# A mixture-of-experts stage whose experts branch at the fifth weight tile, with split weight tiles that come free one at a time

## The chip, the cores and the metric

The kernel runs on one core of one Trainium2 chip and computes one whole layer of a diffusion backbone in one launch. The metric is the device time of that launch in microseconds (us). Three runs of the kernel before gave 2664.49, 2667.15 and 2668.33 us; the median, 2667.15, is the time before. The trace comes from one more execution.

PE is the matrix engine, DVE the vector engine, ACT the scalar engine, POOL the GpSimd engine, and SP the engine that issues most DMAs.

## What the kernel computes

A layer has a mixing part (neighbourhood attention and a convolution), which the change does not touch, and a mixture of experts on 2048 tokens of 1024 numbers, all in float32:

```python
g_idx = argmax(h @ w_rg + b_rg)                     # one of 4 groups
top_v, top_i = top_k(e_logits in that group, 2)     # 2 of its 8 experts
gate = p_group * softmax(top_v)
for e in range(32):                                 # rows sorted by expert
    xb = h[rows of e]                               # rows x 1024
    y = (silu(xb @ w_g[e]) * (xb @ w_u[e])) @ w_d[e]  # 1024 x 512, 512 x 1024
    out[rows of e] += y * gate
x = x_mid + g2 * out
return rmsnorm(x, final_norm)
```

How many rows an expert gets is known only at run time.

## The kernel before

`stage_moe` takes the 32 experts in order. An expert has 12 weight tiles of 128 x 1024 float32, 512 KB each: tiles 0 to 7 are the gate and up weights (`w_gu`), tiles 8 to 11 the down weights (`w_d`). SP issues the DMA of each (`fetch`, L1207) into a ring of 9 raw buffers `ws`. A raw tile is then split in two by `load` (L1212): ACT copies it to a rounded high part `wh` (L1222), and DVE subtracts that from the raw tile for the low part `wl` (L1224); POOL does the subtraction for 2 of the 12 tiles, gate/up tile 1 and down tile 2 (`POOL_LO`). The split tiles have three sets of buffers, by the letter in their names: five pairs `wha/wla` for gate/up tiles 0 to 2, five `whb/wlb` for tiles 3 to 7, and four `whd/wld` for the down tiles.

A float32 product is three matmuls: high by high, high by low, low by high. `block` (L1316) computes an expert's first 128 rows: 24 matmuls of 512 columns for tiles 0 to 3 into one PSUM tile `g`, 24 for tiles 4 to 7 into another, each closed by a SiLU on ACT (L1342) and a gated product on DVE (L1343), then 24 for the down tiles into `y`. `turn` transposes the 512 intermediate numbers per row, half at a time, and splits them into `pah` and `pal`; `rows_t` does the same for the next expert's rows, between the gate/up and the down matmuls. `split` (L52, L53) is the helper: the high part on ACT, the low part on DVE, out of PSUM. Which load stands behind which matmul is written out by hand in the dictionary `mid`, and the order in the program is the order on each engine, since the stage runs under `manual_schedule`. An engine works its list in order: an instruction that waits holds up all that stands behind it.

An expert can have more than 128 rows. `nblk[e]` counts blocks of 64. After `block`, PE, ACT, DVE and POOL branch (`more{e}`, L1499): for at most two blocks they only run `results` (the PSUM tiles `y` times a gain, added to DRAM rows by POOL's indirect DMA); for three, `block64` computes the further 64 rows against the same 12 tiles; for four, `second` runs `block` again; beyond that there is a loop. In this input, among experts 0 to 30, 19 have at most two blocks ("usual" below), 9 have three (experts 2, 4, 10, 14, 15, 16, 19, 26, 29) and 3 have four (12, 13, 27). Expert 31 is written apart, with the final norm behind it. The further rows `yo` are gathered for each expert that has some, and transposed in every expert at L1375 (`rows_t64`), by the hook `mid[10]`.

Of the kernel before, what the change touches and what calls it, by code (L numbers as in the profile page):

```python
# [21 lines left out]
GB, DB, WS = 5, 4, 9  # L22
# [4 lines left out]
POOL_LO = (("g", 1), ("d", 2))  # L27
# [14 lines left out]
class Net:  # L42
# [827 lines left out]
    def stage_out(self, merging):  # L870
# [9 lines left out]
        with ExitStack() as st:  # L880
# [228 lines left out]
            def first_rows(m, pb):  # L1109
# [15 lines left out]
                self.x0 = _f(self.wr_pool.tile([128, D], F32R, name="wha", bufs=GB))  # L1125
# [81 lines left out]
    def fetch(self, d, e, n):  # L1207
        f = self.wr_pool.tile([128, D], F32, name="ws", bufs=WS)
        self.SY.dma_start(out=f, in_=self.I["w_gu" if d is self.WG else "w_d"][e, n])
        self.raw[d is self.WG, e, n] = f  # L1210

    def load(self, d, e, n):  # L1212

        A, V, P = self.A, self.V, self.P
        gu = d is self.WG
        if (gu, e, n) not in self.raw:
            self.fetch(d, e, n)
        f = self.raw.pop((gu, e, n))
        pool, tag, bufs = (self.wr_pool, "a", GB) if gu and n < 3 else (self.wl_pool, "b", GB) if gu else (self.wl_pool, "d", DB)
        h = pool.tile([128, D], F32R, name="wh" + tag, bufs=bufs)  # L1220
        l = pool.tile([128, D], F32R, name="wl" + tag, bufs=bufs)
        A.activation(out=h, in_=f, func=AF.Copy)  # L1222
        eng = P if ("g" if gu else "d", n) in POOL_LO else V
        eng.tensor_tensor(out=l, in0=f, in1=_f(h), op=OP.subtract)  # L1224
        d.setdefault(e, {})[n] = h, l

    def first_weights(self):

        self.wr_pool = self.ctx.enter_context(self.tc.tile_pool(name="mr", bufs=1, side="right"))
        self.WG, self.WD, self.raw = {}, {}, {}  # L1230
        for n in range(3):
            self.load(self.WG, 0, n)
        for n in range(3, 8):
            self.fetch(self.WG, 0, n)
        for n in range(4):
            self.fetch(self.WD, 0, n)

    def stage_moe(self):
# [4 lines left out]
        with ExitStack() as st:  # L1243
            cp = st.enter_context(tc.tile_pool(name="mc", bufs=1))
            wp = self.wl_pool = st.enter_context(tc.tile_pool(name="mw", bufs=1))
            sp = self.wr_pool
            p = st.enter_context(tc.tile_pool(name="mt", bufs=2))
            tp = st.enter_context(tc.tile_pool(name="mtp", bufs=4, space=PSUM))
            gp = st.enter_context(tc.tile_pool(name="mgp", bufs=2, space=PSUM))
# [26 lines left out]
            yo = cp.tile([128, D], F32, name="yo")  # L1276
            P.memset(yo, 0.0)
            yt = cp.tile([128, D], F32, name="yt")
            yq = [yp.tile([128, CW], F32, name=f"y{half}") for half in range(2)]
            yw = cp.tile([64, D], F32, name="yw")  # L1280
            WG, WD, load = self.WG, self.WD, self.load
# [5 lines left out]
            def rows_t(x, to=None):  # L1287

                xh, xl = to or [p.tile([128, 8, 128], F32R, name=n, bufs=1) for n in ("xh", "xl")]

                def step(b):
                    t = tp.tile([128, 4, 128], F32, name="t")
# [23 lines left out]
            def block(e, x, idx, w, mid={}, between=(), z=None):  # L1316


                xh, xl = x
                at = lambda n: [f() for f in mid.get(n, ())]  # L1320

                def turn(half):
                    t = tp.tile([128, 4, 128], F32, name="t")
                    for k in range(2):
                        T.transpose(t[:, k, :], ps[:, half * 256 + k * 128:half * 256 + (k + 1) * 128], ident)
                    ks = slice(2 * half, 2 * half + 2)
                    self.split(pah[:, ks, :], pal[:, ks, :], t[:, 0:2, :])

                for half in range(2):
                    q = gp.tile([128, 2, 256], F32, name="g")  # L1330
                    for n in range(4):
                        h, l = WG[e][4 * half + n]
                        for j in range(2):
                            k, c = 2 * n + j, slice(j * CW, (j + 1) * CW)
                            T.matmul(q, xh[:, k, :], h[:, c], start=(k == 0), stop=False)  # L1335
                            T.matmul(q, xh[:, k, :], l[:, c], start=False, stop=False)  # L1336
                            T.matmul(q, xl[:, k, :], h[:, c], start=False, stop=(k == 7))  # L1337
                        at(4 * half + n)
                        if half and n == 2:
                            turn(0)  # L1340
                    a = ps[:, half * 256:half * 256 + 256]
                    A.activation(out=a, in_=q[:, 0, :], func=AF.Silu)  # L1342
                    V.scalar_tensor_tensor(out=a, in0=a, scalar=w, in1=q[:, 1, :], op0=OP.mult, op1=OP.mult)  # L1343
                for f in between:
                    f()
                y, qs = yt, yq
                for k in range(4):
                    h, l = WD[e][k]
                    for half, q in enumerate(qs):
                        c = slice(half * CW, (half + 1) * CW)  # L1350
                        T.matmul(q, pah[:, k, :], h[:, c], start=(k == 0), stop=False)
                        T.matmul(q, pah[:, k, :], l[:, c], start=False, stop=False)
                        T.matmul(q, pal[:, k, :], h[:, c], start=False, stop=(k == 3))
                    if k == 0:
                        turn(1)
                    at(8 + k)

                def results():
                    V.tensor_tensor(out=y[:, 0:CW], in0=qs[0], in1=g2r[:, 0:CW], op=OP.mult)
                    A.activation(out=y[:, CW:D], in_=qs[1], func=AF.Copy)  # L1360
                    P.tensor_tensor(out=y[:, CW:D], in0=y[:, CW:D], in1=g2r[:, CW:D], op=OP.mult)
                    if z is None:
                        add_rows(y, 128, idx)
                    else:
                        V.tensor_tensor(out=y, in0=y, in1=z, op=OP.add)

                return results

            def rows_t64(x):

                for b in range(2):
                    t = tp.tile([128, 4, 128], F32, name="t")
                    ks = slice(4 * b, 4 * b + 4)
                    for k in range(4):
                        T.transpose(t[:, k, :], x[:, (b * 4 + k) * 128:(b * 4 + k + 1) * 128], ident)  # L1375
                    self.split(xo[:, ks, 0:64], xo[:, ks, 64:128], t[:, :, 0:64])

            def block64(e, idx, w, z=None, y=None, aside=()):


                def pair(q, s, h, l, first, last):

# [319 lines left out]
```

## Time and profile before

| | us |
|---|---|
| median of three runs | 2667.15 |
| the profiled execution | 2663.24 |
| its span, first to last instruction | 2661.2 |
| experts 0 to 30, first gate matmul 1731.64 to that of expert 31 | 848.1 |
| from expert 31 to the end of the span | 81.4 |
| PE busy in the span | 2421.3 (91%) |
| DVE busy | 1702.9 (64%) |
| ACT busy | 1217.4 (46%) |
| POOL busy | 956.1 (36%) |

The shares are means over stages that differ. The change touches the stretch from 1731.64 on, and so the rows below are of that stretch. In a row of a timeline the first number is the start and the second the duration; consecutive instructions of one form are put together with their count (x2). Matmuls overlap their neighbours by part of their duration, so steps are read from start to start. The bracket at the end is the time that the engine idled before the row, and what ended the idling. [...]

### The profile page before, as it was taken

The numbers are of one execution on the slowest core, as the hardware profiler recorded it, in microseconds if no ns is written. First come the engines' busy times: TensorE is split into PE (matmuls) and PEld (weight loads), VectorE is DVE, ScalarE is ACT, GpSimd is POOL, SyncE is SP. The second block draws the span as 40 slices with busy tenths as digits, with TensorE's granted clock in tenths as the row PEclk, the third lists the DMA queues.
The fourth block names the chain that finished last, engine by engine and source line by source line (L and its number), as shares of the span: only waits on it lengthen the run. The fifth ranks groups of instructions, "written<-read, shape, count | busy, mean of one in ns | idle before, by whom it ended". The sixth has DMA issues, their size and how long they took to land. (4 is left out here: it accounts for less than half of the span.)

```text
span 2661.2 us, 36529 instructions
## 1 busy us (share of the span) xinstructions
PE 2421.3 (91%) x12776; PEld 2005.7 (75%) x12776; DVE 1702.9 (64%) x2687; ACT 1217.4 (46%) x2089; POOL 956.1 (36%) x691
## 2 busy tenths in 40 slices
PE   7997999999999999999889999789999998988992
PEld 3786877788878898888877888677777777777772
DVE  7652079999303033887676666676876667777676
ACT  6511111111125211888763333365765556666564
POOL 2300022332110213667533333344454444444442
PEclk9998999999999999999999999899999999999996
DMA  6488534222434357786736343588897678898786
GB/s 247 148 286 189 151 115 138 66 81 98 153 121 152 102 175 229 166 180 146 161 106 210 127 141 113 186 269 294 301 358 258 208 228 279 264 337 304 242 280 240
DMA packets 239637, 522.16 MB, mean 196 GB/s; under 512 B 31383, under 2 KB 122663, under 8 KB 235751
## 3 DMA queue, kind: packets, MB, share of 16 engines
q1 hardware_dynamic: 177431, 403.50, 43.2%
q0 software_dynamic: 24992, 92.06, 15.3%
q10 hardware_dynamic: 36912, 22.92, 3.3%
q8 instruction: 148, 2.42, 0.4%
q14 instruction: 154, 1.26, 0.2%
HBM read 409.76 MB, written 131.43 MB: 203 GB/s over the span
## 5 line engine op out<-in xcount | busy, mean ns | idle before, releaser
L242 PE MATMUL pj<-hTh,wl 128*128 128x512 f32 x1216 | 475.0, 391 | 9.3 <-POOL wl L173 9.3
L240 PE MATMUL pj<-hTh,wh 128*128 128x512 f32 x1216 | 476.1, 392 | 3.2 <-ACT wh L172 3.2
L241 PE MATMUL pj<-hTl,wh 128*128 128x512 f32 x1216 | 475.9, 391 | 0.0
L300 DVE SCALAR_TENSOR_TENSOR cacc<-u,conv_w,cacc 128x2048 f32<-128x2048 f32 x120 | 311.3, 2618 | 1.9
L173 POOL TENSOR_TENSOR wl<-wf,wh 128x1024 fp32r<-128x1024 f32 x32 | 103.5, 3235 | 559.9 <-ACT wh L172 559.9
L242 PEld LDWEIGHTS pj<-hTh,wl 128*128 128x128 f32 x1216 | 232.6, 191 | 55.8 <-POOL wl L173 11.0
L240 PEld LDWEIGHTS pj<-hTh,wh 128*128 128x128 f32 x1216 | 232.6, 191 | 48.4 <-ACT wh L172 3.6
L241 PEld LDWEIGHTS pj<-hTl,wh 128*128 128x128 f32 x1216 | 232.3, 191 | 44.3 <-DVE hTl L232 0.4
L1224 DVE TENSOR_TENSOR wlb<-ws,whb 128x1024 fp32r<-128x1024 f32 x160 | 184.2, 1214 | 0.0
L1224 DVE TENSOR_TENSOR wld<-ws,whd 128x1024 fp32r<-128x1024 f32 x96 | 151.5, 1605 | 20.9 <-ACT whd L1222 20.4
L1222 ACT ACTIVATE whb<-ws 128x1024 fp32r<-128x1024 f32 x160 | 154.8, 1046 | 0.0
L1224 POOL TENSOR_TENSOR wla<-ws,wha 128x1024 fp32r<-128x1024 f32 x32 | 85.2, 2661 | 187.6 <-ACT wha L1222 180.5
L53 DVE TENSOR_TENSOR PTl<-t,PTh 128x384 fp32r<-128x384 f32 (+2 forms) x256 | 122.4, 519 | 31.0 <-ACT PTh L52 28.4
L1335 PE MATMUL g<-wha,xh 128*128 128x512 f32 x192 | 87.8, 457 | 59.1 <-ACT whb L1222 24.1
L700 DVE CUSTOM_DVE_ANT_0 sb<-s,W 128x640 f32<-128x640 f32 (+1 forms) x128 | 113.8, 890 | 37.0 <-PE s L696 14.1
L1224 DVE TENSOR_TENSOR wla<-ws,wha 128x1024 fp32r<-128x1024 f32 x64 | 104.4, 1631 | 43.5 <-ACT wha L1222 39.1
L318 ACT ACTIVATE sg<-pj 128x512 f32<-128x512 f32 x64 | 37.9, 595 | 204.5 <-PE pj L242 103.0
L1224 POOL TENSOR_TENSOR wld<-ws,whd 128x1024 fp32r<-128x1024 f32 x32 | 92.9, 2903 | 98.7 <-ACT whd L1222 98.7
L1222 ACT ACTIVATE whd<-ws 128x1024 fp32r<-128x1024 f32 x128 | 128.0, 1051 | 0.0
L1335 PE MATMUL g<-whb,xh 128*128 128x512 f32 x320 | 127.7, 399 | 0.0
L1337 PE MATMUL g<-whb,xl 128*128 128x512 f32 x320 | 125.3, 392 | 0.0
L1336 PE MATMUL g<-wlb,xh 128*128 128x512 f32 x320 | 124.8, 390 | 0.0
(417 smaller groups left out, 6304.6 us busy)
## 6 DMA issues: line engine op xcount, KB each, us to landing
ws<-in_w_gu_dram SPq DMA_DIRECT2D x256, 512.0 KB
ws<-in_w_d_dram SPq DMA_DIRECT2D x128, 512.0 KB
wf<-in_w_in_dram SPq DMA_DIRECT2D x32, 512.0 KB
wmod<-in_w_mod_t_dram SPq DMA_DIRECT2D x32, 512.0 KB
vw_s<-v_s ACTq DMA_DIRECT2D x128, 128.0 KB
v<-vw_s POOLq DMA_DIRECT2D x32, 512.0 KB, 3.9
kk<-k_s POOLq DMA_DIRECT2D x16, 576.0 KB, 9.2
h_s<-xn SPq DMA_DIRECT2D x17, 512.0 KB
```

The lines of the kernel that those rows point to most:

```text
L53: self.V.tensor_tensor(out=lo, in0=src, in1=_f(hi), op=OP.subtract)
L173: P.tensor_tensor(out=l, in0=f, in1=_f(h), op=OP.subtract)
L240: T.matmul(p[:, :n], w[0][:, k, :], hTh[c][:, k, :], start=(k == 0), stop=False)
L241: T.matmul(p[:, :n], w[0][:, k, :], hTl[c][:, k, :], start=False, stop=False)
L242: T.matmul(p[:, :n], w[1][:, k, :], hTh[c][:, k, :], start=False, stop=(k == 7))
L300: V.scalar_tensor_tensor(out=acc, in0=u[:, t:t + S], scalar=cw[:, i, t:t + 1], in1=acc, op0=OP.mult, op1=OP.add)
L700: V.tensor_tensor_reduce(out=sb[:, 0:w], in0=s.rearrange("p a b -> p (a b)")[:, 256:256 + w], in1=t.rearrange("p a b -> p (a b)"), scale=1 ...
L1222: A.activation(out=h, in_=f, func=AF.Copy)
L1224: eng.tensor_tensor(out=l, in0=f, in1=_f(h), op=OP.subtract)
L1335: T.matmul(q, xh[:, k, :], h[:, c], start=(k == 0), stop=False)
L1336: T.matmul(q, xh[:, k, :], l[:, c], start=False, stop=False)
L1337: T.matmul(q, xl[:, k, :], h[:, c], start=False, stop=(k == 7))
```

## The change

An expert becomes two pieces of program. The head computes gate/up tiles 0 to 3 and, behind their first tile, writes the results of the expert before. Then comes a branch: an expert of at most two blocks runs `arm` without an argument, one of three `arm(..., Few)`, one of four or more `arm(..., Many)`. An arm does the rest of the expert. In `Few` and `Many` the further rows meet each weight tile soon after the first 128 rows did, in PSUM tiles of their own. The weights 12e + n of all experts now form one sequence; tile t is split into pair t mod 8, so a pair is written again as soon as the tile 8 before it has been used for the last time. There are 20 raw buffers (9 until the stage starts). Five tiles of the next expert are split ahead (`AHEAD`) where two were. `yo` has two buffers, and its transposes are in `Few` and `Many` alone. The same two of an expert's 12 tiles go to POOL (1 and 10). More than four blocks run the slow loop, which this input does not reach. Expert 31 keeps its form, with its loads listed anew.

```diff
-GB, DB, WS = 5, 4, 9
+NP, NP0, WS, WS0 = 8, 4, 20, 9
+AHEAD = 5
-POOL_LO = (("g", 1), ("d", 2))
+POOL_LO = (1, 10)
...
+    def load(self, hl=None):
+        f = self.raw.pop(self.loaded)
+        h, l = hl or self.pairs[self.loaded % NP]
+        self.A.activation(out=h, in_=f, func=AF.Copy)
+        eng = self.P if self.loaded % 12 in POOL_LO else self.V
+        eng.tensor_tensor(out=l, in0=f, in1=_f(h), op=OP.subtract)
+        self.idle.append(f)
+        self.W[self.loaded] = h, l
+        self.loaded += 1
...
+            def arm(e, x, steps, other=None):
+                o, w = other, slot[:, e, 1:2]
+                turns[0] = 0
+                if o:
+                    o.start(e)
+                for n in range(4, 8):
+                    gate_up(gb, x, e, n)
+                    if n == 6:
+                        turn(ps, pah, pal, 0)
+                    if n == 7:
+                        act(gb, ps, 1, w)
+                    if o:
+                        o.gate_up(gc, e, n - 4)
+                    self.load()
+                if o:
+                    o.act(e, gc, 0)
+                for f in steps:
+                    f()
+                if o:
+                    for n in range(4, 8):
+                        o.gate_up(ga, e, n)
+                        self.load()
+                        if n == 5:
+                            turn(ps, pah, pal, 1)
+                        if n == 6:
+                            o.turn(0)
+                    o.act(e, ga, 1)
+                for k in range(4):
+                    down(yq, pah, pal, e, k)
+                    if not o and k == 0:
+                        turn(ps, pah, pal, 1)
+                    if o and k == 1:
+                        o.turn(1)
+                    if not o:
+                        self.load()
+                        if k == 2:
+                            self.load()
+                if o:
+                    for k in range(4):
+                        o.down(qo, e, k)
+                        if k == 1:
+                            self.load()
...
+            def results_of(e):
+                results(yt, yq, ids[:, e:e + 1])
+                n = beyond(e, (mybir.EngineType.Pool, mybir.EngineType.Activation, mybir.EngineType.DVE))
+                with tc.If(n > 2):
+                    with tc.If(n <= 3) as few:
+                        results64(yw, qo, ido[0:64, e:e + 1])
+                    with few.Else():
+                        results(yw, qo, ido[:, e:e + 1])
...
+            for e in range(NE - 1):
+                while self.idle and self.fetched < 12 * NE:
+                    self.fetch()
+                hint(f"usual{e}", nblk[e] <= 2)
+                for n in range(4):
+                    gate_up(ga, x, e, n)
+                    if n < 3:
+                        self.load()
+                    if n == 0:
+                        rest(e + 1)
+                        if e + 2 < NE:
+                            xg[e + 2] = new(e + 2)
+                        if e:
+                            results_of(e - 1)
+                act(ga, ps, 0, slot[:, e, 1:2])
+                nx, steps = rows_t(xg.pop(e + 1))
...
+                with tc.If(nblk[e] <= 2, label=f"usual{e}", preferred_fallthrough_block=True):
+                    hint(f"further{e}", nblk[e] > 2)
+                    arm(e, x, steps)
+                with tc.If(nblk[e] > 2, label=f"further{e}", preferred_fallthrough_block=True):
+                    with tc.If(nblk[e] <= 3):
...
+                        arm(e, x, steps, Few)
+                    with tc.If(nblk[e] > 3, label=f"many{e}", preferred_fallthrough_block=True):
...
+                        arm(e, x, steps, Many)
```

Of the changed code, `gate_up`, `down` and `turn` are the matmuls and transposes of `block` as functions of a tile (L1347 to L1349 and L1355), `act` its SiLU and product (L1371, L1372), `Few` the products of `block64` on the further 64 rows, `Many` those of `block` on the further 128.

On DVE, before, a usual expert ends like this, from the transposed rows of the next expert (`xl`) to its results (`yt`); `wld` is its last down tile, `wla` tile 0 of the next expert:

```order
L53 TENSOR_TENSOR xl<-t,xh 128x512 [waits Activation_49] x2
L53 TENSOR_TENSOR pal<-t,pah 128x256 [waits Activation_49]
L1224 TENSOR_TENSOR wld<-ws,whd 128x1024 [waits DMAHW1_49,Activation_49]
L1224 TENSOR_TENSOR wla<-ws,wha 128x1024 [waits DMAHW2_49,Activation_49]
L53 TENSOR_TENSOR xo<-t,xo 128x4x64 [waits Activation_49] x2
L1499 COMPARE_AND_BRANCH
L1359 TENSOR_TENSOR yt<-y_15941,g2r 128x512 [waits DMASW1_49,DVE_49,DMASW6_49,PE_49,DMASW7_49,Pool_49]
```

After the change the same stretch of a usual expert's arm on DVE reads as follows; `wl_15372`, `wl_15376`, `wl_15378` and `wl_15972` are tiles 0, 2, 3 and 4 of the next expert (tile 1 is POOL's), and the last rows are the end of the arm:

```order
L54 TENSOR_TENSOR xl<-t_15951,xh 128x512 [waits Activation_49]
L54 TENSOR_TENSOR xl<-t_15949,xh 128x512 [waits Activation_49]
L54 TENSOR_TENSOR pal<-t_15950,pah 128x256 [waits Activation_49]
L1222 TENSOR_TENSOR wl_15372<-ws_4_15366,wh_15371 128x1024 [waits DMAHW1_49,Activation_49]
L1222 TENSOR_TENSOR wl_15376<-ws_6_15368,wh_15375 128x1024 [waits DMAHW3_49,DVE_49,Activation_49]
L1222 TENSOR_TENSOR wl_15378<-ws_7_15369,wh_15377 128x1024 [waits DMAHW4_49,DVE_49,Activation_49]
L1222 TENSOR_TENSOR wl_15972<-ws_8_15370,wh_15971 128x1024 [waits DMAHW5_49,DVE_49,Activation_49]
L1637 UNCONDITIONAL_BRANCH
L1637 UNCONDITIONAL_BRANCH [waits DVE_49]
L1640 COMPARE_AND_BRANCH
```

Two splits of weights stood behind `pal`, then those of the further rows and `yt`; now four splits of weights stand there, and `yt` has moved into the next head.

On PE, before, the rows from the last down matmul of an expert past its branch (the code for more rows is left out) to the first gate matmul of the next:

```order
L1352 MATMUL y_15942<-wld,pah 128x512
L1353 MATMUL y_15942<-whd,pal 128x512
L1499 COMPARE_AND_BRANCH
...
L1499 UNCONDITIONAL_BRANCH [waits PE_49]
L1494 REGISTER_ALU
L1698 BRANCH_PREFETCH_HINT
L1454 UNCONDITIONAL_BRANCH
L1335 MATMUL g<-wha,xh 128x512 [waits DVE_49,PE_49,Activation_49]
```

After the change the same place, from the end of the usual arm past the arms for further rows:

```order
L1348 MATMUL y_15947<-wl_15989,pah 128x512
L1349 MATMUL y_15947<-wh_15988,pal 128x512
L1637 UNCONDITIONAL_BRANCH
L1637 UNCONDITIONAL_BRANCH [waits PE_49]
L1640 COMPARE_AND_BRANCH
...
L1640 UNCONDITIONAL_BRANCH [waits PE_49]
L1589 UNCONDITIONAL_BRANCH
L1606 REGISTER_ALU
L1849 BRANCH_PREFETCH_HINT
L1347 MATMUL g_15952<-wh_15371,xh 128x512 [waits DVE_49,Activation_49]
```

PE passes two conditional branches per expert where it passed one, and the first gate matmul behind the join still stands behind waits on DVE and ACT.

In the middle of an expert with three blocks PE now runs from the last matmul of the head past the usual arm to the transposes of the further rows:

```order
L1349 MATMUL g_15952<-wh_15988,xl 128x512
L1637 COMPARE_AND_BRANCH
...
L1637 UNCONDITIONAL_BRANCH
L1637 UNCONDITIONAL_BRANCH [waits PE_49]
L1640 COMPARE_AND_BRANCH
L1641 COMPARE_AND_BRANCH
L1606 REGISTER_ALU
L1849 BRANCH_PREFETCH_HINT
L1407 MATMUL t_15950<-ident,yo_15938 128x128 [waits DMASW5_49,DVE_49]
```

Those transposes stood in `mid[10]`, behind the third down tile; they now stand directly behind the branch, with a wait on DVE, and the gate matmuls of tiles 4 to 7 behind them.

## Rows read from the trace of the kernel before

**Rows 1.** What PE waited for in the stretch 1731.6 to 2579.76
```profile
PE g L1335 <- ACT whb L1222: 24.1, 8, 3.2
PE g L1335 <- PEq L1499: 15.9, 5, 4.3
PE y L1353 <- DVE pal L53: 10.8, 17, 1.1
PE g L1335 <- ACT yt L1360: 10.6, 13, 0.8
```

**Rows 2.** Timeline of PE: start, duration, instruction, idle before and releaser
```profile
1902.06 1.04 PE L1294 MATMUL t<-ident,xg 128*128 128x128 f32 x8
...
1904.32 0.38 PE L1325 MATMUL t<-ident,ps 128*128 128x128 f32 x2
...
1907.29 1.03 PE L1375 MATMUL t<-ident,yo 128*128 128x128 f32 x8
...
1910.54 0.50 PE L1335 MATMUL g<-wha,xh 128*128 128x512 f32 x1 [0.81 <-ACT yt L1360]
...
1974.42 0.75 PE L1335 MATMUL g<-wha,xh 128*128 128x512 f32 x1 [4.26 <-PEq L1499]
```

**Rows 3.** Timeline of ACT in the same expert
```profile
1902.26 0.38 ACT L1342 ACTIVATE ps<-g 128x256 f32<-128x256 f32 x1 [0.96 <-PE g L1337]
...
1902.70 1.09 ACT L52 ACTIVATE xh<-t 128x512 fp32r<-128x512 f32 x2
...
1904.78 0.38 ACT L52 ACTIVATE pah<-t 128x256 fp32r<-128x256 f32 x1 [1.00 <-ACT xh L52]
...
1906.01 2.00 ACT L1222 ACTIVATE wha<-ws 128x1024 fp32r<-128x1024 f32 x2
...
1909.89 0.60 ACT L1360 ACTIVATE yt<-y 128x512 f32<-128x512 f32 x1 [1.14 <-PEq L1499]
```

**Rows 4.** Windows, the 19 usual experts: length, busy times, clock, DMA share, GB/s; one, and sum
```profile
1910.54:1930.38 19.84, 19.03 (x92) 15.44 (x92) 16.25 (x19) 15.28 (x22) 11.54 (x6) 1.00 1.03 377
...
sum 413.22, PE 377.12 PEld 302.19 DVE 331.84 ACT 278.42 POOL 198.77; mean PE 19.85 PEld 15.90 DVE 17.47 ACT 14.65 POOL 10.46
```

**Rows 5.** Windows, the 9 experts with three blocks: third of them, and sum
```profile
1974.42:2009.85 35.43, 32.45 (x161) 25.78 (x161) 21.87 (x31) 21.53 (x35) 11.95 (x7) 0.95 0.78 249
...
sum 315.97, PE 285.56 PEld 225.85 DVE 208.68 ACT 190.35 POOL 142.74; mean PE 31.73 PEld 25.09 DVE 23.19 ACT 21.15 POOL 15.86
```

**Rows 6.** Windows, the 3 experts with four blocks
```profile
2030.11:2068.71 38.60, 37.52 (x176) 30.22 (x177) 21.81 (x26) 17.77 (x27) 15.42 (x9) 1.00 0.74 248
...
sum 118.93, PE 115.16 PEld 92.26 DVE 64.34 ACT 52.01 POOL 46.16; mean PE 38.39 PEld 30.75 DVE 21.45 ACT 17.34 POOL 15.39
```

**Rows 7.** Windows, the gate and up products of two experts, 43 matmuls each
```profile
1890.69:1900.45 9.76, 9.76 (x43) 7.95 (x43) 8.83 (x9) 8.86 (x10) 5.69 (x5) 1.00 0.95 246
1974.42:1985.72 11.30, 11.30 (x43) 9.10 (x44) 9.74 (x9) 8.66 (x10) 2.92 (x3) 0.85 1.04 332
```

**Rows 8.** Timeline of DVE in two usual experts
```profile
1878.50 4.54 DVE L1224 TENSOR_TENSOR wld<-ws,whd 128x1024 fp32r<-128x1024 f32 x2
...
1899.24 2.35 DVE L1224 TENSOR_TENSOR wld<-ws,whd 128x1024 fp32r<-128x1024 f32 x2
...
1903.33 1.29 DVE L53 TENSOR_TENSOR xl<-t,xh 128x512 fp32r<-128x512 f32 x2 [0.17 <-ACT xh L52]
...
1905.20 0.42 DVE L53 TENSOR_TENSOR pal<-t,pah 128x256 fp32r<-128x256 f32 x1 [0.58 <-ACT pah L52]
...
1908.43 0.78 DVE L53 TENSOR_TENSOR xo<-t,xo 128x256 fp32r<-128x256 f32 x2
```

**Rows 9.** Timeline of POOL beside them
```profile
1879.44 2.52 POOL L1224 TENSOR_TENSOR wld<-ws,whd 128x1024 fp32r<-128x1024 f32 x1 [3.79 <-ACT whd L1222]
...
1899.87 3.99 POOL L1224 TENSOR_TENSOR wld<-ws,whd 128x1024 fp32r<-128x1024 f32 x1 [3.48 <-ACT whd L1222]
...
1908.08 2.67 POOL L1224 TENSOR_TENSOR wla<-ws,wha 128x1024 fp32r<-128x1024 f32 x1 [4.23 <-ACT wha L1222]
```

More of the change, by code (lines that the diff above doesn't have):

```diff
@@ L1238, in stage_moe @@
+        self.room(self.wr_pool, WS0, NP0)
+        for _ in range(3):
+            self.fetch()
+        for _ in range(3):
+            self.load()
+        while self.idle:
+            self.fetch()
     def stage_moe(self):
@@ L1314, in put_rows @@
                 return P.indirect_dma_start(out=self.out[:, :], out_offset=IO(ap=idx, axis=0), in_=y, in_offset=None)
[L1316 to L1367, printed above, removed]
@@ new lines, in three, with turn @@
+            def three(q, sh, sl, h, l, first, last):
+                T.matmul(q, sh, h, start=first, stop=False)
+                T.matmul(q, sh, l, start=False, stop=False)
+                T.matmul(q, sl, h, start=False, stop=last)
+            def turn(src, hi, lo, half):
+                t = bank()
+                for k in range(2):
+                    T.transpose(t[:, k, :], src[:, half * 256 + k * 128:half * 256 + (k + 1) * 128], ident)
+                ks = slice(2 * half, 2 * half + 2)
+                if lo is None:
+                    self.split(hi[:, ks, 0:64], hi[:, ks, 64:128], t[:, 0:2, 0:64])
+                else:
+                    self.split(hi[:, ks, :], lo[:, ks, :], t[:, 0:2, :])
@@ new lines, in pair, with gate_up64 @@
+            def pair(q, s, h, l, first, last):
+                lo = lambda: T.matmul(q[0:64], s[:, 0:64], l, start=False, stop=False)
+                if last:
+                    lo()
+                T.matmul(q, s, h, start=first, stop=last)
+                if not last:
+                    lo()
+            def gate_up64(q, e, n, a=0, b=256):
+                for j in range(2):
+                    k = 2 * (n % 4) + j
+                    hw, lw = (z.rearrange("p (j x c) -> p j x c", j=2, x=2)[:, j, :, a:b] for z in weight(e, n))
+                    pair(q, xo[:, k, :], hw, lw, k == 0, k == 7)
@@ L1467, in stage_moe, with hint @@
+            def hint(label, stays):
+                tc.mark_branch_hint_location(label, hint=stays, engines=[mybir.EngineType.PE])
             st.enter_context(tc.manual_schedule())
[L1468 to L1470 removed]
             new = lambda e: gather(p.tile([128, D], F32, name="xg", bufs=2), ids[:, e:e + 1])
[L1472 to L1473 removed]
@@ L1521, in stage_moe @@
+            e = NE - 1
+            turns[0] = 0
+            more = [self.home[id(self.idle.pop(0))] for _ in range(8)]
+            more = [pool.tile([128, D], F32R, name=name) for pool, name in more]
+            more = list(zip(more[::2], more[1::2]))
+            while self.fetched < 12 * NE:
+                self.fetch()
+            results_of(e - 1)
             fn = p.tile([128, D], F32, name="xg", bufs=2)
@@ L1529, in read @@
                 xs.append(x)
[L1531 to L1541 removed]
+            for n in range(8):
+                gate_up((ga, gb)[n // 4], x, e, n)
+                if self.loaded < 12 * NE:
+                    self.load(more.pop(0) if self.loaded % 12 >= 8 else None)
+                if n == 6:
+                    turn(ps, pah, pal, 0)
+                if n % 4 == 3:
+                    act((ga, gb)[n // 4], ps, n // 4, slot[:, e, 1:2])
+            rows_t64(yo)
+            gather(yo[0:64], ido[0:64, e:e + 1], self.acc_s)
+            for _ in range(12):
+                read(self.idle.pop(0))
+            read(yos[(e + 1) % 2])
+            for t in ("xh", "xl"):
+                read(_f(cp.tile([128, 8, 128], F32R, name=t)).rearrange("p k c -> p (k c)"))
+            for k in range(4):
+                down(yq, pah, pal, e, k)
+                if k == 0:
+                    turn(ps, pah, pal, 1)
+            results(yt, yq, None, z)
             y = yt
```

350 lines of the change are left out of this document (189 added, 161 removed).

## The prediction, made before the changed kernel ran

> **What bounds the kernel now.** I read the waits of PE first, over experts 0 to 30, since PE is busy for most of the span. The reader is to see that the four largest waits are small against 848 us [rows 1]: 24.1 us in 8 waits on the last weight tiles behind `block64` (3.0 each), 15.9 us in 5 waits of PE's own sequencer at the branch L1499 (3.2 on average), 10.8 us in 17 short waits on `pal`, and 10.6 us in 13 waits of 0.8 on `yt`. Together they are 61.4 us, the most that this change could take from waits.
>
> The timeline of PE says more about the last of these [rows 2]: the first gate matmul of an expert idles 0.81 us and starts at 1910.54. ACT's `yt`, at 1909.89 for 0.60, ends at 1910.49 [rows 3]. That matmul does not read `yt`. So behind a branch's join PE waits until the other engines are through the branch, whatever the operands. Here this costs little, because ACT and DVE have almost nothing left to do when PE ends an expert.
>
> The windows give the sums: 19 usual experts 413.2 us, a good one 19.84 [rows 4]; 9 with three blocks 316.0 [rows 5]; 3 with four 118.9 [rows 6].
>
> **A usual expert after the change.** I count from its first gate matmul, T = 0, with the durations of the expert that begins at 1890.69 [rows 7].
>
> PE: of 19.84, the 0.81 before the first matmul goes, and the transposes of `yo` (1.03 in the row, about 0.8 without overlap) go too [rows 2]. PE's own work is then 18.2 us. Gate/up matmuls end at 11.4 (1902.06 less 1890.69), the second `turn` comes at 13.6.
>
> ACT: the SiLU starts at 11.6 for 0.38; then the copy of tile 11, about 1.0 (two take 2.00), to 12.95; two `xh`, 1.09, to 14.05; `pah` to 14.5 [rows 3]. Now five copies stand there (tiles 12 to 16), where three did: they end at 15.5, 16.45, 17.4, 18.35 and 19.3.
>
> DVE: a low part takes 1.18 undisturbed (two in 2.35), the two `xl` 1.29, `pal` 0.42 [rows 8]. Tile 11 runs 12.95 to 14.15, `xl` to 15.4, `pal` to 15.8, tile 12 to 17.0; tile 14 waits for its copy at 17.4 and ends at 18.6; tiles 15 and 16 end at 19.75 and 20.9. The order shows four low parts behind `pal` before the arm ends, and the next expert's first gate matmul behind a wait on DVE and ACT. By the `yt` row that wait is for the end of their arms, not for tile 12 alone. So the next expert begins at 20.9 at the earliest, 2.7 us after PE's last matmul. This wait takes the place of the 0.81.
>
> What is queued behind that matmul is all of PE's next head; ACT's and DVE's next loads stand behind the same join. The results, the reads of the count and the gather of the next rows now lie in the head, where ACT has only three copies and two results in 5.5 us of gate matmuls; I cost them at nothing, and at about 1 us an expert if that cover fails.
>
> **POOL against DVE.** POOL makes the low parts of tiles 10 and 13. The rows show what that does to DVE: with POOL's subtraction begun at 1879.44 between two of DVE, DVE's two took 4.54; with DVE in a run, they took 2.35 and POOL's took 3.99 instead of 2.52. Operations of DVE that read PSUM run beside POOL untouched (`xo` 0.78, in POOL's 2.67) [rows 8, 9]. So one low part waits for the other to end.
>
> In the new order POOL has tile 10 from 11.5 to 14.0 while DVE waits for ACT, so tile 11 ends at 15.2, `pal` at 16.9 (PE stalls about 1.2 for it, as it does now 17 times [rows 1]); POOL starts tile 13 at 16.45, beside `xl` and `pal`, and ends at 19.0; tiles 12, 14, 15, 16 of DVE end at 20.15, 21.3, 22.5 and 23.65. If the first collision is missed, DVE is in tile 12 until 17.0 and pauses until 17.4 for ACT; POOL, waiting since 16.45, goes in there and ends at 19.5; DVE ends at 23.05. The ends are 20.9 (no collision) and 23.65 (both); I take 23.05, since each order leaves DVE a pause in which POOL's operation is ready.
>
> [...]
>
> **The clock.** With 23.05 PE idles 4.8 us before an expert (3.6 where it stalled for `pal`). After an idle of 4.26 [rows 2] 43 gate/up matmuls took 11.30 at a granted clock of 0.85, against 9.76 at 1.00 [rows 7]: 1.54 us, at the lower of the two levels for part of it. I charge 1.54 to each expert that follows a usual one, and none to one that follows an expert with further rows, where the last loads stand in front of the last down matmuls. That is 11 usual experts and expert 0, 6 with three blocks and 1 with four.
>
> **Experts with further rows.** Three blocks: the cold example takes 35.43 [rows 5]; less 1.54 and less the 3.0 behind it that goes [rows 1] it is 30.9. The new middle adds a wait: the transposes of `yo` stand behind DVE's first product, which comes after SiLU; from the end of the gate matmuls to the end of that product I take 1.1 (0.2 to start, read from 1902.06 to 1902.26, 0.38 [rows 2, 3], 0.42 for a DVE pass of this size [rows 8]). So 32.0 warm, 33.5 cold. Four blocks: PE's 37.52 [rows 6] and 1.1, 38.6 warm.
>
> PE's branches: the jump at the end of an expert now lies under the wait for DVE. The 12 experts with further rows jump over the usual arm in the middle, in the open. Five of the 19 jumps of before missed; at that rate 3.2 of 12 miss, at 3.2 less the 1.1 that is idle anyway: 7 us. Bounds are 0 and 25 (all 12).
>
> **The sum.** Usual: 7 x 23.05 + 12 x 24.6 = 456.6, against 413.2: +43.4. Three blocks: 6 x 33.5 + 3 x 32.0 = 297.0, against 316.0: -19.0. Four: 3 x 38.6 + 1.5 = 117.3, against 118.9: -1.6. Branches +7. Together +29.8 on the profiled execution's 2663.24, which has 2.0 us around its span: 2693. The median of the runs is 3.9 us higher, and nothing of the sum hangs on that. Expert 31 and the tail (81 us) keep their work; I leave 3 us either way.
>
> **Rivals.**
>
> *DVE keeps ahead of POOL.* If no collision falls on the last tiles, a usual expert takes 20.9, PE idles 2.7 and its clock holds. Then 19 x 20.9 is 397.1 (-16.1), three blocks 9 x 32.0 = 288 (-28.0), four 115.8 (-3.1), branches +7: -40, 2623. The place is the start of POOL's tile 13, and it decides from a mean of 22.5 a usual expert, clock included: there the losses equal the 14 that the others save. For it speaks the 3.99 row, against it the 4.54 row and DVE's pauses.
>
> *The join does not hold PE.* If the first matmul needs only its own tiles, PE runs on: 19 x 18.5 = 351.5 (-61.7), with -28.0, -3.1 and +7: -86, 2577. A good expert moved 377 GB/s at a DMA share of 1.03 in 19.84 us [rows 4]; should that be the rate, 19 x 19.84 = 377 and the time is 2603. Against this rival stands the `yt` row.
>
> *Every jump of PE is paid.* With 12 misses, 25 in place of 7: 2711. The other engines jump too, over shorter pieces; 1 us an expert at the join adds 31: 2738 with some of it hidden. [...]
>
> **Chances.** The forecast, with sizes between 2673 and 2710, 0.40; paid jumps and worse 0.17; DVE ahead of POOL 0.25; the join open 0.08; a mixture that ends level 0.10. What a measurement can tell from no change is 0.2%, 5.3 us either way. So slower 0.57, the same 0.10, faster 0.33. As cases of both signs hold much of the chance, the range goes from 2612, below the first rival, to 2738; the forecast's own is 2673 to 2725.
>
> **What would show it.** In the profile after: PE's idle before the first gate matmul (L1347) behind a usual expert, 3.6 to 4.8 us, ended by DVE `wl`; DVE's four low parts behind `pal`, one of them over 3 us beside POOL's; a mean clock under 0.95 in the stretch; 0 us on the last weight tiles behind three blocks; about 1.1 before L1407. Idle under 2.9 there and a usual expert near 21 would make the forecast wrong by the collisions; idle ended by a weight tile's own split, with an expert near 18.5, would make it wrong by the join.

## The result, and the profile after

The changed kernel took 2828.98 us (median of 4 runs, 2823.3 to 2835.91) against 2667.16 before: a ratio of 1.0609, 95% interval 1.0584 to 1.0634. It is slower by 162 us. The prediction had the direction, slower, but 2693 us, and its range ended at 2738.

The profiled execution took 2828.34 us with a span of 2826.6. Experts 0 to 30 now run from 1729.28 to 2744.43, which is 1015.2 us in place of 848.1. The rest of the span is as it was (82.2 in place of 81.4 behind them). These rows are the windows of the 31 experts, before and after; the mean granted clock, third from the end, is 0.97 before and 0.91 after:

```profile
1731.64:2579.76 848.12, 777.83 (x3717) 620.30 (x3717) 604.86 (x711) 520.78 (x772) 387.67 (x191) 0.97 0.83 279
1729.28:2744.43 1015.15, 813.97 (x3397) 625.71 (x3397) 640.26 (x642) 508.51 (x703) 381.23 (x193) 0.91 0.70 235
```

What PE waited for in that stretch (total, times, longest), where [rows 1] had 61.4 us in its four rows:

```profile
PE g L1347 <- DVEq L1640: 57.2, 19, 4.3
PE t L1355 <- DVE po L1432: 36.4, 9, 4.1
PE y L1348 <- POOL wl L1222: 35.2, 7, 5.2
PE g L1348 <- POOLq L1637: 17.1, 3, 7.1
PE g L1348 <- POOLq L1641: 10.4, 2, 6.6
PE y L1349 <- DVE pal L54: 9.6, 12, 0.9
PE t L1407 <- DVEq L1637: 8.5, 8, 1.1
```

A name such as DVEq L1640 means that the wait ended when DVE's sequencer passed the join at that line. None of the four waits of [rows 1] is the largest any more, and the seven rows here add up to 174 us. PE was also busy for 36 us more, though the trace has fewer matmuls (3397 in place of 3717): at the lower clock a matmul takes longer. The granted clock has two levels in the traces of the two kernels, 0.50 and 1.00 of full speed: before, in the slow example of [rows 7] gate matmuls start 0.43 us apart from 1974.96 to 1977.10, at 0.50, and 0.23 apart from 1978.38 on, at 1.00.

The windows by kind of expert answer to [rows 4 to 6]. First the usual ones (one behind an expert with further rows, one behind a usual one, the sum of the 19), then those with three blocks (one behind a usual expert, the third of a chain of three, the sum), then the sum of those with four:

```profile
1821.87:1848.31 26.44, 20.33 (x84) 15.97 (x85) 23.84 (x19) 15.07 (x21) 15.91 (x9) 0.87 0.92 297
...
1939.01:1963.98 24.97, 19.93 (x84) 15.66 (x85) 18.48 (x17) 14.58 (x19) 9.96 (x5) 0.91 0.89 304
...
sum 485.22, PE 383.26 PEld 299.96 DVE 389.08 ACT 280.86 POOL 235.87; mean PE 20.17 PEld 15.79 DVE 20.48 ACT 14.78 POOL 12.41
```

```profile
1779.84:1821.87 42.03, 35.27 (x145) 26.29 (x145) 20.54 (x25) 18.86 (x28) 9.39 (x5) 0.90 0.61 215
...
2265.76:2315.43 49.67, 35.79 (x145) 26.32 (x145) 21.44 (x27) 19.25 (x30) 15.61 (x8) 0.86 0.47 155
...
sum 392.78, PE 314.46 PEld 233.66 DVE 186.95 ACT 169.28 POOL 105.45; mean PE 34.94 PEld 25.96 DVE 20.77 ACT 18.81 POOL 11.72
```

```profile
sum 137.15, PE 116.25 PEld 92.10 DVE 64.23 ACT 58.37 POOL 39.91; mean PE 38.75 PEld 30.70 DVE 21.41 ACT 19.46 POOL 13.30
```

Usual experts cost 485.2 where they cost 413.2, three blocks 392.8 for 316.0, four 137.2 for 118.9: 72.0, 76.8 and 18.2 us more. Three places account for most of this.

**The join.** The expert that begins at 1939.01 ends like this on PE, DVE and POOL (start, duration, instruction, idle before):

```profile
1959.35 0.40 PE L1349 MATMUL y<-wh,pal 128*128 128x512 f32 x1
1963.98 0.77 PE L1347 MATMUL g<-wh,xh 128*128 128x512 f32 x1 [4.23 <-DVEq L1640]
```

```profile
1953.43 2.13 DVE L1222 TENSOR_TENSOR wl<-ws,wh 128x1024 fp32r<-128x1024 f32 x1 [0.47 <-ACT wh L1220]
...
1956.68 0.41 DVE L54 TENSOR_TENSOR pal<-t,pah 128x256 fp32r<-128x256 f32 x1
1957.02 6.76 DVE L1222 TENSOR_TENSOR wl<-ws,wh 128x1024 fp32r<-128x1024 f32 x4
```

```profile
1956.90 2.39 POOL L1222 TENSOR_TENSOR wl<-ws,wh 128x1024 fp32r<-128x1024 f32 x1 [2.42 <-ACT wh L1220]
```

PE's last down matmul starts at 1959.35. DVE's last four low parts, begun at 1957.02, took 6.76 in place of about 4.6 (1.15 for each, as in the five of 5.76 us in the experiment with no low part on POOL); POOL had begun its own at 1956.90. The low part of tile 11, at 1953.43, took 2.13 beside POOL's of tile 10 (2.40 from 1952.08), where [rows 8] had 2.35 for two. The four end at 1963.78, and PE starts 0.20 later, after an idle of 4.23. The last of them is tile 4 of the next expert, for which PE has no use yet. Then the head begins at the lower clock, 0.50 from 1963.98 to 1968.90: the first matmul takes 0.77 (0.50 behind the idle of 0.81 in [rows 2]), and the mean granted clock of the expert that begins here is 0.89.

**The splits in front of a product.** In an expert with three blocks (1779.84), ACT, DVE and PE around the second half of the further rows:

```profile
1804.13 2.01 ACT L1220 ACTIVATE wh<-ws 128x1024 fp32r<-128x1024 f32 x2
...
1806.29 1.07 ACT L1220 ACTIVATE wh<-ws 128x1024 fp32r<-128x1024 f32 x1
...
1807.40 1.08 ACT L1220 ACTIVATE wh<-ws 128x1024 fp32r<-128x1024 f32 x1
1808.50 0.59 ACT L1429 ACTIVATE yw<-g 64x512 f32<-64x512 f32 x1
1811.77 0.42 ACT L1431 ACTIVATE yw<-yw 64x256 f32<-64x256 f32 x1 [2.68 <-DVE yw L1430]
```

```profile
1807.40 2.41 DVE L1222 TENSOR_TENSOR wl<-ws,wh 128x1024 fp32r<-128x1024 f32 x1 [0.52 <-ACT wh L1220]
...
1809.93 1.21 DVE L1222 TENSOR_TENSOR wl<-ws,wh 128x1024 fp32r<-128x1024 f32 x1
1811.07 0.67 DVE L1430 TENSOR_TENSOR yw<-g,yw 64x512 f32<-64x512 f32 x1
1812.22 0.48 DVE L1432 SCALAR_TENSOR_TENSOR po<-yw,slo 64x256 f32<-64x256 f32 x1 [0.48 <-ACT yw L1431]
```

```profile
1808.31 0.40 PE L1349 MATMUL y<-wh,pal 128*128 128x512 f32 x1
1812.75 0.69 PE L1355 MATMUL t<-ident,po 128*128 128x128 f32 x2 [4.04 <-DVE po L1432]
```

PE turns from the further rows' gate/up matmuls to the down tiles at 1805.74. ACT copies weights (`wh`) from 1804.13 on and reaches their result only at 1808.50. DVE's addition (L1430) stands behind two more weight splits, one of them 2.41 long beside POOL's, and starts at 1811.07. PE has done two down tiles and idles 4.04 us for `po`; the slow clock follows (0.50 from 1812.75 to 1815.75; 0.69 for these two transposes, where [rows 2] had 0.38 for two).

**POOL's queue.** POOL and PE in the usual expert behind that one:

```profile
1826.18 2.30 POOL L1328 DMA_INDIRECT acc_s<-yt,ids  x1 [0.28 <-POOL yt L1384]
1827.94 2.99 POOL L1395 TENSOR_TENSOR yw<-yw,g2r 64x1024 f32<-64x1024 f32 x1
1838.03 2.02 POOL L1328 DMA_INDIRECT acc_s<-yw,ido  x1 [7.09 <-DMA acc_s<-yt,ids]
1839.54 5.21 POOL L1222 TENSOR_TENSOR wl<-ws,wh 128x1024 fp32r<-128x1024 f32 x2
```

```profile
1842.48 0.80 PE L1348 MATMUL y<-wl,pah 128*128 128x512 f32 x1 [4.98 <-POOL wl L1222]
```

The results of the expert before are now in the head. POOL adds the first 128 rows at 1826.18 and multiplies the further rows, but their add waits 7.09 us for the DMA of the first add, until 1838.03. Behind it stand POOL's two low parts. PE waits 4.98 us for the first of them (down tile 2). In a chain of experts with further rows PE does not even reach a low part of POOL; it waits until POOL has passed the branch:

```profile
2234.17 0.79 PE L1348 MATMUL g<-wl,xh 128*128 128x512 f32 x1 [5.70 <-POOLq L1637]
```

### The profile page after: what moved, and what is told of

The parts are those of the page before. It is cut to its first block, busy times and chain, and to the rows that moved or that the text cites. A ratio compares the mean times of both kernels' runs of the same rounds, so it can differ in the third digit from the quotient of the medians.

```text
span 2826.6 us, 37175 instructions
## 1 busy us (share of the span) xinstructions
PE 2455.5 (87%) x12456; PEld 2009.8 (71%) x12456; DVE 1738.5 (62%) x2616; ACT 1201.9 (43%) x2018; POOL 948.0 (34%) x693
## 5 line engine op out<-in xcount | busy, mean ns | idle before, releaser
L1222 DVE TENSOR_TENSOR wl<-ws,wh 128x1024 fp32r<-128x1024 f32 x317 | 487.9, 1565 | 243.3 <-ACT wh L1220 156.7
L1220 ACT ACTIVATE wh<-ws 128x1024 fp32r<-128x1024 f32 x380 | 386.4, 1054 | 279.2 <-PE g L1415 102.5
L1347 PE MATMUL g<-wh,xh 128*128 128x512 f32 x512 | 220.7, 431 | 67.5 <-DVEq L1640 57.2
L1222 POOL TENSOR_TENSOR wl<-ws,wh 128x1024 fp32r<-128x1024 f32 x63 | 155.0, 2525 | 297.0 <-ACT wh L1220 201.1
L1348 PE MATMUL g<-wl,xh 128*128 128x512 f32 x512 | 214.2, 418 | 27.6 <-POOLq L1637 17.1
L1349 PE MATMUL g<-wh,xl 128*128 128x512 f32 x512 | 212.9, 416 | 0.0
L1347 PEld LDWEIGHTS g<-wh,xh 128*128 128x128 f32 x512 | 104.5, 204 | 104.9 <-issue 80.7
L1348 PE MATMUL y<-wl,pah 128*128 128x512 f32 x248 | 111.6, 450 | 35.2 <-POOL wl L1222 35.2
L1348 PEld LDWEIGHTS g<-wl,xh 128*128 128x128 f32 x512 | 105.2, 205 | 51.3 <-POOLq L1637 18.4
L1349 PEld LDWEIGHTS g<-wh,xl 128*128 128x128 f32 x512 | 103.8, 203 | 24.7
L53 ACT ACTIVATE PTh<-t 128x384 fp32r<-128x384 f32 (+2 forms) x256 | 105.1, 462 | 35.9 <-PE t L725 34.2
```

What stands on the lines that cost most here:

```text
L53: self.A.activation(out=hi, in_=src, func=AF.Copy)
L1220: self.A.activation(out=h, in_=f, func=AF.Copy)
L1347: T.matmul(q, sh, h, start=first, stop=False)
L1348: T.matmul(q, sh, l, start=False, stop=False)
L1349: T.matmul(q, sl, h, start=False, stop=last)
```

## The experiments

All of them ran on chips together with the kernel before, which gave 2668.13 us beside the first four, a median of 2661.86 beside the next three, and 2665.4 beside the last four. Where no number of runs is given, a kernel ran once. Line numbers shift by a few where an edit adds or takes lines.

**The splits behind the product.** In the arms for further rows:

```diff
                         o.gate_up(ga, e, n)
-                        self.load()
...
                     if o and k == 1:
                         o.turn(1)
-                    if not o:
-                        self.load()
-                        if k == 2:
-                            self.load()
+                    self.load()
+                    if not o and k == 2:
+                        self.load()
```

> Only the arms for further rows change: the four splits of the next tiles that stand between the further rows' gate/up matmuls now stand behind their SiLU and product, one behind each down tile. Theory: the 4.0 us that PE idles before the transposes of po, 9 times, 36.4 us in all, come from those splits standing in front of that product on ACT and DVE. Then that wait falls below 1 us each, the slow matmuls behind it (about 1.4 us each) go too, and the time is near 2788. Rival: the splits have to be done before the arm ends in any case, so the idle only moves to the end of the arm, before L1347, where it is 0.7 now: 2820 or more.

Measured: 2777.33 us, 52 less than the change. The waits of PE:

```profile
PE g L1347 <- DVEq L1638: 60.1, 18, 4.3
...
PE t L1355 <- DVE po L1432: 4.2, 1, 4.2
```

The 9 waits on `po` are gone (the one left is in expert 31), nothing of the kind appeared at the end of the arms, and the three-block experts sum to 340.3 us instead of 392.8. The cause holds, and it was worth more than its 36.4 us of waiting.

**No low part on POOL.** `POOL_LO = ()`.

> All low parts go to DVE, none to POOL. Theory: PE's waits on POOL (35.2 us on POOL's low part in the 7 usual experts that follow further rows, 27.5 us on POOL's sequencer in 5 experts with further rows) come from POOL's queue being held by the results of the expert before; with no low part on POOL they vanish, with about 1.4 us of slow matmuls behind each. The join behind a usual expert stays: DVE loses the collision (2.3 us) and gains two low parts (2.4 us). Time near 2755. Rival: DVE is at its capacity and POOL's help was worth its collisions, so that the idle moves to DVE's low parts: 2815 or more.

Measured: 2745.44, 84 less. PE's largest wait, and DVE at the end of a usual arm behind a usual expert:

```profile
PE g L1347 <- DVEq L1640: 58.4, 18, 3.3
...
1947.95 5.76 DVE L1222 TENSOR_TENSOR wl<-ws,wh 128x1024 fp32r<-128x1024 f32 x5
```

The waits on POOL are gone. The usual experts sum to 433.7 instead of 485.2, although DVE now makes all the low parts: those behind a usual expert mostly take 21.7 to 23.3 instead of 23.5 to 26.1, those behind further rows 21.7 to 22.4 instead of 26.5. The expectation left the join as it was. But DVE makes its last five low parts in 5.76 us, where four took 6.76 beside POOL's, and PE idles at most 3.3 there: in this order POOL's help costs DVE more than it takes from it.

**Three tiles ahead.** Two loads move from the end of each arm to the top of the next head (`AHEAD = 3`, two `self.load()` before the head's first `gate_up`, and one each less in the loops of the arms).

> Three tiles are split ahead instead of five: the last two splits of each arm move into the next head, in front of its first matmuls. Theory: behind the join PE waits for the end of DVE's arm, not for the tile that it needs. With two low parts fewer there, DVE ends 2.35 us earlier, PE idles under 2 us instead of 4.25 behind a usual expert, and the head keeps its clock: 12 x 3.6 + 7 x 2.4 = 60 us less, 2769. Rival: PE waits for its own tiles, and later splits make these later: the idle moves into the head or to L1348, 2815 or more.

Measured: 2797.63, 31 less, between the two. The waits, and POOL in the usual expert that begins at 1814.07, behind a three-block one:

```profile
PE y L1348 <- POOL wl L1222: 49.4, 7, 9.6
...
PE g L1347 <- DVEq L1639: 21.8, 11, 2.0
```

```profile
1819.48 6.78 POOL L1328 DMA_INDIRECT acc_s<-yt,ids  x1 [0.28 <-DVE yw L1394]
```

Six of the twelve usual experts behind usual ones take 21.2 to 21.3, as 24.9 less the expected 3.6 gives, and PE idles 2.0 or less in front of them; the others take 22.7 to 25.0. That part of the theory holds. But six of the 7 behind further rows rose from 26.5 to between 27.6 and 31.2 (the seventh fell to 23.1): POOL's add took 6.78 to issue in place of 2.3, and PE waited up to 9.6 us for POOL's low part. Why the issue took longer is not shown; splits of DVE ran beside it, but they also ran beside the one of 2.30 at 1826.18 in the change.

**No add of the further rows.** In `results64` and `results` the call of `add_rows` for the further rows is left out.

> The results of the further rows are computed but not added to the output rows in DRAM (the output lacks them); all else stays. Theory: POOL's second add waits some 7 us for the DMA of the first, and behind it stand POOL's low parts and its step over the branch, for which PE waits. Without it the 62.7 us of waits on POOL fall under 10, with the slow matmuls behind them: near 2752, while the 4.25 us behind usual experts stay. Rival: POOL's low part is late by its collision with DVE: no change, 2829.

Measured: 2789.95, 39 less. The largest wait:

```profile
PE g L1347 <- DVEq L1638: 81.2, 19, 5.1
```

Both waits on POOL are gone, so the second add was their cause, and not the collision alone. The chain of experts 14 to 16 falls from 45.5, 47.7 and 49.7 to 39.7, 40.4 and 40.8. Half of the expected gain did not come: the waits at the join rose from 57.2 to 81.2. The expert behind a three-block one is now early, and meets the join like the others.

**All three edits, and two of them.** The first three experiments in one kernel, and the first two.

> The three edits together: the splits behind the further rows' product, no low part on POOL, three tiles ahead. Theory (join, POOL's queue, splits in front of the product): DVE ends a usual arm at about 19.7 us, PE idles about 1 us behind it, so a usual expert takes 20 (19 x 20 = 380), three blocks 34 (306), four 39 (117): 803 where the kernel before took 848, so 2620 to 2635 in all. Rival: the gains overlap, because each wait that goes uncovers another, or the DMAs become the bound (19.84 us were measured for the 7.48 MB of a usual expert, and now nothing is fetched across the join): 2665 or more.

> Two of the three edits, with five tiles ahead as in the change: splits behind the product, no low part on POOL. Theory: their gains add, since the one is in the arms for further rows and the other in POOL's queue: usual 433 as with no low part on POOL, three blocks 9 x 35 = 315, four 122: 870 in place of 1015, near 2684. Rival: both removed waits of the same experts, and the gains overlap by half: 2715 or more.

Measured: all three 2682.78 (median of 8 runs; 1.0074 times before, 1.005 to 1.0099), two of them 2704.23. All three edits take back 146 us of the change's 162, or 141 with each kernel against the one before that ran beside it. The forecast of 2620 to 2635 was wrong and its rival, 2665 or more, right: not all gains add. The two edits alone, in one kernel, gained 125 us where their single gains make 135; that is between the forecast of 2684 and its rival. Two usual experts of the kernel with all three edits:

```profile
1913.49:1932.96 19.47, 18.50 (x85) 14.54 (x85) 17.43 (x19) 14.59 (x20) 5.76 (x4) 1.00 0.85 302
2419.36:2446.00 26.64, 20.56 (x85) 15.08 (x85) 17.70 (x19) 14.32 (x20) 6.39 (x5) 0.94 0.98 348
```

Seven usual experts take 19.42 to 19.48 like the first, where 20 was forecast. The second, 26.64, has the DMA engines at a share of 0.98, and its ACT waits 2.5 us for a down tile to land. At the joins SP waits before it issues the next DMA, 8.6 us at the longest. The change as it stands has such waits too, 14.6 at the longest: in front of 1963.98 SP issued no weight tile between 1944.46 and 1958.35. What they cost was not tried. Behind further rows, where the head has five splits and the results of two sets of rows, six of the seven usual experts take 22.3 to 25.6. These two are read from rows, and no run took them apart. Nor are they the whole rest: the sums are 409.6 us for the usual experts, 328.9 for three blocks and 128.3 for four, against 413.2, 316.0 and 118.9 before. So what is left of the loss lies in the experts with further rows. In the nine with three blocks PE waits 17.4 us for the transposed rows `xl`, and at the branch in front of the transposes of `yo` 2.1 each, where the change had 1.1; the last row is SP's wait at the joins:

```profile
PE t L1355 <- DVE xl L54: 17.4, 9, 5.9
PE t L1407 <- DVEq L1634: 16.4, 8, 2.9
...
SPq L1637 <- SPq L1637: 220.4, 101, 8.6
```

**Two more operations on DVE.** The kernel of the three edits, with this at the end of a usual arm:

```diff
+                if not o:
+                    for c in (0, DE):
+                        V.tensor_tensor(out=po, in0=g2r[:, c:c + DE], in1=g2r[:, c:c + DE], op=OP.mult)
```

> The kernel of the three edits with two more DVE operations at the end of each usual arm, about 1.3 us together, on a buffer that nobody reads there. Theory: the first gate matmul behind the join waits for the end of DVE's arm, whatever it holds: 19 usual experts lose 1.3 us each, about 25 us, or up to 50 where PE's clock then falls. Rival: PE waits for its own first tiles only, which are split before: no change beyond 5 us.

Measured: 2693.0, 10 us more; the eight runs without them gave 2673.95 to 2687.09. The first gate matmul behind the same expert, without and with them:

```profile
1932.96 0.47 PE L1347 MATMUL g<-wh,xh 128*128 128x512 f32 x1 [0.95 <-DVEq L1637]
```

```profile
1931.11 0.47 PE L1347 MATMUL g<-wh,xh 128*128 128x512 f32 x1 [2.28 <-DVEq L1640]
```

PE idles 1.33 us more, for work that nobody reads. Usual experts of 19.46 become 20.8. Usual experts rose from 409.6 to 424.3 in all, less than 25: the seven behind further rows took only 1.4 more together, and the one of 26.64 took 22.5.

**Four tiles ahead.** The three edits with `AHEAD = 4`.

> The change with the three edits, but four tiles ahead instead of three. Theory: behind a usual expert DVE ends 1.15 us later, so usual experts that follow a usual one go from 19.5 to 20.7 (11 x 1.2 = 13 us more); those behind further rows, whose head on DVE was too long with five splits and the results in it, gain about 1 us each (16 x 1 = 16 us less): about the same, 2675 to 2690. Rival, that the head's length does not matter: 2696.

Measured: 2686.87 (median of 8 runs; 1.0078, 1.0059 to 1.0097), as with three and as expected: usual experts behind usual ones 20.6 instead of 19.5, those behind further rows shorter. The two ends trade.

**Parts of the change in the kernel before.** First the transposes of `yo` in the branch for three blocks only:

```diff
-                mid[10].append(lambda: rows_t64(yo))
+                if not more:
+                    mid[10].append(lambda: rows_t64(yo))
...
+                        rows_t64(yo)
                         block64(e, ido[0:64, e:e + 1], slo[0:64, e, 1:2])
```

> One part of the change alone, put into the kernel before: the transposes of the further rows stand in the branch of three blocks instead of in every expert. Theory: 22 experts lose 8 transposes (0.8 us each on PE, 17.6 us together) and 9 get about 1.1 us of waiting for their split: 8 us less, 2655 to 2660. Rival: the transposes lay beside PE's stalls for pal, and the branch then holds the split and a cold clock: 2667 to 2680.

Measured: 2646.93 (median of 5 runs), 0.9928 times before (0.9895 to 0.996); 18 us less where 8 were forecast. Two of its waits:

```profile
PE y L1353 <- DVE pal L53: 18.6, 16, 1.3
...
PE g L1386 <- DVE xo L53: 6.6, 9, 1.3
```

The wait on `xo` is 0.7 us each, 9 times. Usual experts went from 413.2 to 386.7, three blocks from 316.0 to 327.8, four from 118.9 to 117.6. But the 15.9 us at L1499 [rows 1] are gone in this build; why is not shown. With the slow clock behind such a wait (1.54 us by [rows 7]) they would by themselves explain the gain, by an estimate of 15.9 and 5 x 1.54. So what the transposes alone are worth is not shown.

> The kernel before with all low parts on DVE. If POOL's help is worth less than its collisions there too, as in the change, the 10.8 us on pal go and the usual experts gain: 2645 to 2660. If DVE's 16.2 us of 19.84 are near their limit in the kernel before, two more low parts (2.4 us) make DVE late for the down tiles: 2680 or more.

Measured: 2658.9 (median of 10), 0.9982 (0.9963 to 1.0001): no difference that can be told. POOL's help neither pays nor costs there. PE's waits at the branch are still in this build:

```profile
PE g L1335 <- PEq L1499: 13.0, 5, 2.7
```

> Both edits in the kernel before: the transposes in the branch, and all low parts on DVE, which also loses two splits (0.8 us) in each usual expert. If the two are independent, their differences add; if DVE's load is what the second costs, the first gives it room, and the sum is better than that by up to 10 us.

Measured: 2637.91 (median of 4), 0.9877 (0.9841 to 0.9913). The two differences add, as far as can be told: 27.5 us where the single ones make 25.0. The waits at L1499 are gone here too. This is the fastest kernel of the study, 191 us below the change and 1.2% below the kernel before.

## Why the prediction was wrong

The sum by its own terms, in us:

| term | predicted | measured |
|---|---|---|
| 12 usual experts behind usual ones, with expert 0 | 295.2 | 299.5 |
| 7 usual experts behind further rows | 161.4 | 185.7 |
| 9 with three blocks | 297.0 | 392.8 |
| 3 with four blocks | 117.3 | 137.2 |
| PE's branches | 7 | in the others |

- **The join** was right in mechanism and size. PE waits for the end of DVE's arm: 4.1 to 4.3 us in front of 12 of the 18 experts behind a usual one, predicted 3.6 to 4.8; in front of the other six, whose usual expert itself came late behind further rows, 0.8 to 1.1. The 12 of the first row of the table took 264.6 before, so this cost 35 us, where 31 were forecast. The schedule on DVE ended at 23.05 to 23.65; experts behind usual ones took 23.5 at full clock and 25 to 26 with a slow head, 24.9 on average over the 11, predicted 24.6. The experiment with two unread operations shows that the wait is not for data: PE idled 1.33 us more.
- **POOL against DVE** was right. Both collisions that the prediction described fell, the first on tile 11 (2.13 in place of 1.2) and the second on the last four (6.76 in place of 4.6): POOL begins tile 13 first (1956.90 before 1957.02). That is the order that it put at 23.65; it took 23.05, for an order that misses the first, and the difference is small.
- **The step that failed first is the one on three blocks, "less the 3.0 behind it that goes".** I followed PE's matmuls into the new arm but not ACT's and DVE's lists. The wait did not go; it went into the arm, 4.04 instead of 3.0, because the loads that stood behind the further rows now stand in front of their product. The middle wait that I did foresee was right (8.5 us in 8, predicted 1.1 each). The whole term was 95.8 us too low; moving the loads gave back 52.5 of them. Two more waits in these experts were at nothing in the term: 17.1 us in 3 for POOL's branch, which is the next point, and 8.4 in 9 for `xl` (1.0 at the longest). And matmuls took longer: PE was busy 314.5 us in them, 285.6 before.
- **The second is "I cost them at nothing, and at about 1 us an expert if that cover fails"**, on the results in the head. ACT's cover held: no wait of PE on ACT is among the largest. POOL's queue was not looked at: its second add waits for the first, and with POOL's low parts behind it. This made the 7 usual experts 3.5 us longer each, and in chains of experts with further rows PE waited up to 7.1 us each. Leaving out the add removed all waits on POOL, and 39 us in all.
- **The clock.** The two levels that the prediction speaks of are the 0.50 and 1.00 above. Charging "none to one that follows an expert with further rows" was right for the head (PE idles 0.7 to 0.8 before it) and wrong for the expert: usual ones there have a pause of about 5 us of their own inside, and a mean granted clock of 0.87.
- **PE's branches** were near in size and wrong in place. No jump stalls for 2 to 4 us as five did before, and the one in the middle, at which the 7 us were put, is hidden by the wait on DVE. But behind each of the 12 experts with further rows PE's own sequencer ends an idle of 0.7 to 0.8 at the join, 9.1 us together; these are the 9 behind three blocks:

```profile
PE g L1347 <- PEq L1645: 6.9, 9, 0.8
```

The rival "DVE keeps ahead of POOL" did not occur, nor did the open join. The third rival had its sign right and its place wrong: none of the 12 jumps in the middle stalled. That the direction came out right is in part luck: of the 167 us that the 31 experts lost, the join behind usual experts explains 35, and the largest loss is in the experts with three blocks, for which a gain was forecast.

## What to carry to other kernels

When a piece of program moves, follow the list of every engine that gets it, not the bound engine's alone: a split, an add or a load that was harmless behind a result is a wait in front of it (here 36.4 us in 9 waits on `po`). In this kernel the branch made DVE's last instruction before the join a matter for PE (1.33 us more idle for two operations that nobody reads); so keep the ends of the arms short on the slowest engine. And try the parts of a large change one at a time in the old kernel: one of them, with the transposes in the branch, ran 0.7% faster there, while the whole cost 6%; and read the waits then too, since here PE's waits at a branch went with it.

## What the runs showed of the hardware

- In this change POOL's help cost DVE more than it gave. With two of twelve low parts on POOL, DVE's last four took 6.76 us; with none there, its last five took 5.76. The kernel was 84 us faster without them, in part because nothing then stood behind POOL's adds; in the kernel before, whose order differs, the same edit made no difference that can be told (0.9982).
- Issuing an indirect DMA on POOL took 2.3 us in one usual expert of the change, and 6.78 in one with three tiles ahead; over all 30 adds of the first 128 rows the mean was 2.62 in the change and 3.34 with three tiles ahead. What makes it longer is open.
- The second indirect add to the same tensor in DRAM is ordered behind the landing of the first by a wait of the program. In all 12 experts with further rows POOL stood idle before it, 86.3 us together; in 6 of them the profile names that landing as what ended the idling.
- An indirect add issued at 1826.18 held up what waited for its landing until 1838.03, 11.9 us later.
